# A hybrid attention and convolution backbone on one core: the early output projection one query block sooner with seven row pairs, five convolution chunks on the first token half, and the final norm's weight multiplied ahead of its root

## The chip, the cores and the metric

The kernel runs on one core of a Trainium2 chip. Its engines work side by side, each with a queue of its own: TensorE (PE) for matrix products, VectorE (DVE), ScalarE (ACT) and GpSimd (POOL) for elementwise work, and SyncE (SP), which issues most of the transfers. The metric is the device time of one execution in microseconds; lower is better.

## What is computed

Two layers over 1024 latent tokens of width 1024 with 256 context tokens, cut to what matters here:

```python
# layer 0: windowed attention (|i-j| <= 128) with a sink, gated
h    = rmsnorm(x, g0) * (1 + scale0) + shift0
proj = h @ attn_w_in                      # q, k, v and the gate path z
o    = windowed_attention(rope(q), rope(k), v, k_ctx, v_ctx, sink)
x1   = x + gate0 * ((o * silu(z)) @ attn_w_out)
# layer 1: convolution module, gated
h2   = rmsnorm(x1, g1) * (1 + scale1) + shift1
a, gl, z = split(h2 @ conv_w_in + b, 3)   # three parts of width 2048
u    = depthwise_conv31(a * sigmoid(gl))
u    = silu(layernorm(u))
x2   = x1 + gate1 * ((u * silu(z)) @ conv_w_out)
out  = x2 * rsqrt(mean(x2 * x2) + eps) * final_g
```

Everything is in float32. Each large product is made of three products of float32r parts (high by high, high by low, low by high), so an operand is first split into a high part (a copy on ACT) and a low part (a subtraction on DVE or POOL).

## The kernel before, in words

**The attention.** Sixteen heads with eight query blocks of 128 tokens make 128 steps. In each step PE computes the scores of the next block (`scores`, three times two matmuls), then "fills" with `FILL` = 12 matmuls of other work, then transposes the probabilities of the present block (`transposes`), and after every fourth block multiplies them with the values (`pv`). Between scores and transposes lies the softmax: a masked maximum on DVE (it writes `sc`), the exponential on ACT, a reciprocal on DVE and a multiplication on POOL. The transposed probabilities leave PSUM as `pthi` (ACT) and `ptlo` (DVE). The filling work is taken from a queue, `fillq`: the input projections of later heads, the last of which is the gate path `z` of head 15.

**The early output projection.** The output projection (`proj_attn`) contracts over eight row pairs, a pair being two heads, for four blocks of rows in each of four passes. It needs, for each pair, the weight `wo`, its low part `wol` (made earlier by `low_parts` and kept in DRAM) and the gated head outputs `ozf` read back from DRAM. In head 15 the projection begins early as filling work: at query blocks `EARLY_FROM - 2` and `EARLY_FROM - 1` the loads of the first two pairs are issued, at `EARLY_FROM` their split, and `early_proj` joins the queue, frees the pages of the layer's input and does the first two of the four row blocks for `EARLY_ROWS` pairs, 12 matmuls a pair. The main loop then starts those pairs at the third row block (line 724).

**The way to the convolution.** Behind each pass `evac0` adds the residual and collects sums of squares. When the second half of the tokens (512) is complete, eight closures `turn_in` are put on a list, `later`: each transposes a slice of the normalised rows on PE, and DVE and ACT make `hf`, `h2h` and `h2l` of it, the operands of the next projection.

**The convolution's projection.** `b_mm(i, half)` multiplies chunk `i` (128 output channels) of the weight with one half of the tokens: 24 matmuls of 512 columns. Chunks come in the order gl 0, a 0, gl 1, a 1, gl 2, and so on, with z chunks mixed in from the ninth pair on. Before, chunks 0 to 3 (`2 * EARLY`) run on the first token half, then the same chunks on the second, and from chunk 4 on both halves of a chunk follow each other. While chunks 2 and 3 run on the first half, `b_mm` takes the second half's `turn_in` closures from `later`. A gl chunk goes through a sigmoid into a page that all channel tiles share (`sigp`, one half each for the two token halves); an a chunk is multiplied with it into `ubuf`, where the depthwise convolution reads it (`conv_dve`: 32 products and sums on DVE per channel tile; `conv_pool`: the odd taps, products on ACT, sums on POOL). The layer norm's mean is a matmul of the sum of all channel tiles, `vsum`.

**The final norm.** `evac1` handles one block of 128 rows after the last projection: gate product (DVE, out of PSUM), residual (DVE or POOL), `Square` with its sum on ACT, then, when both column halves are there, `rstd_of`: `ms` (DVE), a square root (ACT) and five small DVE instructions up to `r`. Two DVE instructions multiply each half with `r` and the weight `fg`, and SP stores each half.

**What sets the order.** From line 1064 on only PE keeps the program's order. The order on DVE, ACT, POOL and SP is set when the kernel is built, by a planner that simulates the engines and prefers what stands earlier in the program; the engines then keep to it. Tiles lie in 45 pages of 4 KB a partition, handed out in the order in which they were freed; PSUM has two score tiles, two `psg` banks and two `pso` banks.

Of the kernel before, what the change touches and what calls it, by code (L numbers as in the profile page):

```python
# [11 lines left out]
AF = mybir.ActivationFunctionType  # L12
ALU = mybir.AluOpType
# [20 lines left out]
FILL = 12  # L34
DEFER = 6
EARLY = 2
EARLY_ROWS = 6
EARLY_FROM = 4
KEEP = 8
BYBLOCK = 3  # L40
ZV = (1, 4, 7)
# [52 lines left out]
def backbone_kernel(  # L94
# [8 lines left out]
    V, A, G, PE, SY = (InOrder(tc, e) for e in (nc.vector, nc.scalar, nc.gpsimd, nc.tensor, nc.sync))  # L103
# [29 lines left out]
    def ps_g():  # L133
        return ps.tile([P, 512], F32, tag="g", name=nm("psg"), bufs=2)
# [3 lines left out]
    def ps_og():  # L138
        flip[0] ^= 1
        return ps_o() if flip[0] else ps_g()  # L140
# [4 lines left out]
    def small(shape, dt=F32, name="sm", bufs=2):  # L145
        return cpool.tile(shape, dt, tag=f"{name}", name=nm(name), bufs=bufs)

    def act(out, in_, func, **kw):
        return A.activation(out=out, in_=in_, func=func, **kw)

    def tt(eng, out, a, b, op):
        return eng.tensor_tensor(out=out, in0=a, in1=b, op=op)

    def stt(out, in0, scalar, in1, op0, op1):
        return V.scalar_tensor_tensor(out=out, in0=in0, scalar=scalar, in1=in1, op0=op0, op1=op1)
# [39 lines left out]
    def mm3(o, wh, wl, rh, rl, start, stop):  # L195
        PE.matmul(o, wh, rh, start=start, stop=False)
        PE.matmul(o, wh, rl, start=False, stop=False)
        PE.matmul(o, wl, rh, start=False, stop=stop)
# [293 lines left out]
    for pr in range(NPR):  # L492
        a, b = 2 * pr, 2 * pr + 1
# [143 lines left out]
    def proj_attn():  # L637
# [32 lines left out]
        def ahead(i, nl, ns):  # L670
            while todo["load"] <= min(i + nl, len(seqB) - 1):
                load(todo["load"])
                todo["load"] += 1
            while todo["split"] <= min(i + ns, len(seqB) - 1):
                split(todo["split"])
                todo["split"] += 1

        def block(s, kk, b, acc, w, o):
            for e in range(2):
                lh, ll = (t[:, e, b * P:b * P + P] for t in o)  # L680
                for a, c in ((lh, w[0]), (lh, w[1]), (ll, w[0])):
                    PE.matmul(acc, a, c[:, e], start=kk == 0 and e == 0 and a is lh and c is w[0],
                              stop=kk == NK - 1 and e == 1 and a is ll)
                    yield
# [6 lines left out]
        banks = {4: ps_g(), 5: ps_g()}  # L691
        for i in range(EARLY_ROWS):
            ahead(i, EA, min(1, EARLY_ROWS - 1 - i))
            for b in range(2):
# [7 lines left out]
        for i, (s, kk) in enumerate(seqB):  # L702
# [9 lines left out]
            if i >= len(seqB) - BYBLOCK:  # L712
# [10 lines left out]
                continue  # L723
            for b in range(2 if i < EARLY_ROWS else 0, 4):
                run(block(s, kk, b, acc[b], w, o))
# [192 lines left out]
    def run(gen):  # L918
        for _ in gen:
            pass  # L920
# [12 lines left out]
    def enqueue(key):  # L933
        fillq.append((key, job(key)))
# [148 lines left out]
    for i, (h, qb) in enumerate(steps):  # L1083
        if qb == 0:
            for n in (() if h % 4 == 3 else (h + 1,) if h % 4 or not h else (h, h + 1)):
                enqueue(("z", n))
                if n + 1 < NH:
                    enqueue(("q", n + 1))
        if (h, qb) == (NH - 1, EARLY_FROM - 2):
            run(lows)  # L1090
        if h == NH - 1 and EARLY_FROM - 2 <= qb < EARLY_FROM:
            next(projA)
        if (h, qb) == (NH - 1, EARLY_FROM):
            next(projA)
# [68 lines left out]
    border = []  # L1163
# [35 lines left out]
    def v2(ap):  # L1199
        return ap.rearrange("p (a b) -> p a b", b=256)  # L1200
# [83 lines left out]
    def conv_unit(j, n0, n1, whole=None):  # L1284

        if (j, n0) not in conv:
            st = {"done": False, "us": None, "n0": n0, "n1": whole or n1}
            conv[(j, n0)] = st
            if whole and whole > n1:
                conv[(j, n1)] = st  # L1290
            pq.append(conv_pool(j, n0, whole or n1))
        opened.add((j, n0))
        dq.append(conv_dve(j, n0, n1))
# [13 lines left out]
    def advance(dt):  # L1307
        pump(pq, "p", dt, P_COST)
        pump(dq, "d", dt, D_COST)


    def vh(j, half):
        return vpg[j][:, :, half * 256:half * 256 + 256]
# [46 lines left out]
    late = deque()  # L1360
# [42 lines left out]

    def b_mm(i, half):
        wh, wl = wsB.need(i)
        if i < 2 * EARLY or late:
            o = ps_g()
        else:
            o = ps_og()
        sl = slice(half * 512, half * 512 + 512)  # L1410
        for kt in range(KT):
            mm3(o, wh[:, kt], wl[:, kt], H2h[(half, kt)], H2l[(half, kt)], kt == 0, kt == KT - 1)
            if kt % 2 and later and i >= EARLY:
                later.popleft()()
            if kt == 3:
                advance(2.6)
        kind, j = border[i]
        cur[0] = i
        bias = vt[:, boff[kind] + j:boff[kind] + j + 1]
        if kind == "gl":  # L1420
            with tc.high_priority():
                act(sigt[(j, half)], o, AF.Sigmoid, bias=bias)
        elif kind == "a":
            u = ubuf[j % 4]
            while any(k[0] == j - 4 for k in opened):
                advance(2.6)
            with tc.high_priority():
                stt(u[:, :, 8 + half * 256:264 + half * 256], v2(o), bias, v2(sigt[(j, half)]), ALU.add, ALU.mult)
            if j < EARLY:
                conv_unit(j, *((248, 512) if half else (0, 248)))  # L1430
            elif half:
                conv_unit(j, 0, 512 if j < JSPLIT else 256, 512)
        else:
            zs = zbuf[j % len(zbuf)][:, half]
            with tc.high_priority():
                act(zs, o, AF.Silu, bias=bias)
            if (j, half) in yready:
                tt(V if j % 8 in ZV else G, vh(j, half), vh(j, half), v2(zs), ALU.mult)
            else:
                spilled.add((j, half))  # L1440
                SY.dma_start(out=zsd[j, :, sl], in_=zs)
        late_now()
        if not late:
            advance(2.6)
# [7 lines left out]
    def late_now():  # L1452

        if ("a", NJ - 1) not in border[:cur[0]]:
            return
        late0.append(1)
        if len(late0) == LATE_FROM:
            while dq or pq:
                advance(2.6)
            late.append(1)  # L1460
        if late:
            ln_run(5.2, len(late) in LN_AT)
            late.append(1)
# [4 lines left out]
    def tok_rows(ap, h, b):  # L1468

        n0 = h * 256 + b % 2 * P  # L1470
        return ap.rearrange("(n a) d -> a n d", a=2)[b // 2, n0:n0 + P]
# [29 lines left out]
    def evac1(s, b, acc):  # L1501
        h, m = subs[s]
        ns = slice(m * 512, m * 512 + 512)
        if b % 2 == 0:
            x2[(m, b // 2)] = pg.alloc(F32, [2, 512], "x2")
            x2["xr"] = pg.alloc(F32, [2, 512], "xr")
        if m == 0:
            x2[b] = small([P, 2], name="ssf", bufs=8)
        t, ss, xr = x2[(m, b // 2)][:, b % 2], x2[b], x2["xr"][:, b % 2]
        SY.dma_start(out=xr, in_=tok_rows(x1d, h, b)[:, ns])  # L1510
        tt(V, t, acc, gbc[:, ns], ALU.mult)
        tt(G if b % 2 and s < len(subs) - 1 else V, t, t, xr, ALU.add)
        if b % 2:
            pg.free(x2["xr"])
        junk = hp.alloc(F32, None, "junk")
        act(junk[:, 0:512], t, AF.Square, accum_out=ss[:, m:m + 1])
        hp.free(junk)
        if m == 0:
            return
        tt(V, ss[:, 0:1], ss[:, 0:1], ss[:, 1:2], ALU.add)  # L1520
        r = rstd_of(ss[:, 0:1], D, 1)
        dst = tok_rows(out[0], h, b)
        for m in range(2):
            t = x2[(m, b // 2)]
            os = slice(m * 512, m * 512 + 512)
            stt(t[:, b % 2], t[:, b % 2], r, fg[:, os], ALU.mult, ALU.mult)
            SY.dma_start(out=dst[:, os], in_=t[:, b % 2])
            if b % 2:
                used.append(t)
# [82 lines left out]

    run(projA)
    pg.free(*gbc0)
    for i in range(2 * EARLY):
        b_mm(i, 0)
        wsB.load()
        wsB.split()
        wsB.load()
    for i in range(2 * EARLY):  # L1620
        b_mm(i, 1)
        wsB.done(i)
        wsB.load()
    for i in range(2 * EARLY, len(border)):
        if i == len(border) - 1:
            next(projB)
        wsB.need(i)
        wsB.load()
        wsB.split()
        wsB.load()  # L1630
        b_mm(i, 0)
        if i == len(border) - 1:
            pg.free(*h2pg[0])
            next(projB)
        b_mm(i, 1)
        wsB.done(i)
        if border[i] == ("a", NJ - 1):
            zbuf.append(sigp)
# [3 lines left out]
    fg = pg.alloc(F32, [1024], "fg")  # L1642
# [52 lines left out]
```

## Time and profile before

| | |
|---|---|
| median of 3 runs | 1778.02 us (1777.82 to 1778.15) |
| the profiled execution | 1782.36 us, its span 1780.1 us |
| granted TensorE clock, mean | 0.991 |
| moved by DMA | 242.43 MB, mean 136 GB/s |

The span runs from the first to the last instruction of the profiled execution. All work is recorded under line 88, the helper that issues every instruction, so the profile is read by tile names (`psg`, `h2l_page`, `sc`), engines and time. A row of the timeline has the start, the duration, the engine, the operation, the output and inputs, and in brackets the idle time of the engine before it with what ended it. A matmul's duration overlaps the next one's, so PE's pace is read from start to start. A row of the waits has the total, the number and the longest.

### The profile page before, as it was taken

The numbers are of one execution on the slowest core, as the hardware profiler recorded it, in microseconds if no ns is written. First come the engines' busy times: TensorE is split into PE (matmuls) and PEld (weight loads), VectorE is DVE, ScalarE is ACT, GpSimd is POOL, SyncE is SP. The second block draws the span as 40 slices with busy tenths as digits, with TensorE's granted clock in tenths as the row PEclk, the third lists the DMA queues.
The fourth block names the chain that finished last, engine by engine and source line by source line (L and its number), as shares of the span: only waits on it lengthen the run. The fifth ranks groups of instructions, "written<-read, shape, count | busy, mean of one in ns | idle before, by whom it ended". The sixth has DMA issues, their size and how long they took to land. (4 is left out here: it accounts for less than half of the span.)

```text
span 1780.1 us, 23728 instructions
## 1 busy us (share of the span) xinstructions
PE 1722.9 (97%) x8383; PEld 1419.1 (80%) x8383; DVE 1203.3 (68%) x2165; ACT 885.6 (50%) x1540; POOL 780.4 (44%) x610
## 2 busy tenths in 40 slices
PE   5999999999999999999999999999999999999997
PEld 2788888788887888788888887888888888787886
DVE  6766774667555664666314269999999999866823
ACT  6555543455344453444433445654656565456730
POOL 0244343333423343432100247998988789120300
PEclk8999999999999999999999999999999999999999
DMA  9334443444234443336776733111121212377881
GB/s 311 102 81 139 143 127 93 125 147 145 80 116 131 142 150 93 114 100 206 256 248 241 260 94 102 29 48 36 36 83 36 73 46 71 120 245 237 311 281 48
DMA packets 195322, 242.43 MB, mean 136 GB/s; under 512 B 11798, under 2 KB 126790, under 8 KB 195204
## 3 DMA queue, kind: packets, MB, share of 16 engines
q1 hardware_dynamic: 188516, 230.10, 39.8%
q10 hardware_dynamic: 6688, 10.83, 2.6%
q8 instruction: 66, 1.08, 0.3%
q14 instruction: 52, 0.43, 0.1%
HBM read 188.70 MB, written 41.69 MB: 129 GB/s over the span
## 5 line engine op out<-in xcount | busy, mean ns | idle before, releaser
L88 POOL TENSOR_TENSOR odd_half<-odd_half,prod_half 128x513 f32<-128x513 f32 (+2 forms) x252 | 317.9, 1269 | 20.8 <-ACT prod_half L88 7.3
L88 POOL TENSOR_TENSOR wlo_page<-wraw_page,whi_page 128x1024 fp32r<-128x1024 f32 x71 | 173.8, 2449 | 153.0 <-ACT whi_page L88 115.6
L88 POOL TENSOR_SCALAR p_page<-p_page,sc 128x640 f32<-128x640 f32 (+1 forms) x128 | 104.2, 815 | 307.7 <-DVE sc L88 280.2
L88 PE MATMUL psg<-hh_page,whi_page 128*128 128x512 f32 x600 | 237.6, 396 | 0.0
L88 PE MATMUL psg<-hh_page,wlo_page 128*128 128x512 f32 x600 | 236.3, 394 | 0.0
L88 PE MATMUL psg<-hl_page,whi_page 128*128 128x512 f32 x600 | 236.0, 393 | 0.0
L88 ACT ACTIVATE prod_half<-ubuf,dww 128x513 f32<-128x513 f32 (+2 forms) x252 | 165.0, 674 | 108.6 <-POOL odd_half L88 104.4
L88 PE MATMUL psg<-h2l_page,whi_page 128*128 128x512 f32 x456 | 180.6, 396 | 1.8 <-DVE h2l_page L88 1.8
L88 PE MATMUL psg<-h2h_page,whi_page 128*128 128x512 f32 x456 | 181.5, 398 | 0.0
L88 PE MATMUL psg<-h2h_page,wlo_page 128*128 128x512 f32 x456 | 180.1, 395 | 0.0
L88 DVE SCALAR_TENSOR_TENSOR pss<-ubuf,wsum,pss 128x512 f32<-128x512 f32 (+3 forms) x270 | 172.3, 671 | 0.3
L88 DVE SCALAR_TENSOR_TENSOR pss<-ubuf,dww,pss 128x512 f32<-128x512 f32 (+3 forms) x270 | 172.1, 671 | 0.3
L88 ACT ACTIVATE p_page<-p_page,sc 128x641 f32<-128x641 f32 (+1 forms) x128 | 102.9, 804 | 91.8 <-DVE sc L88 87.3
L88 ACT ACTIVATE pthi<-pss 128x640 fp32r<-128x640 f32 (+1 forms) x144 | 88.7, 616 | 104.7 <-PE pss L88 98.0
L88 DVE TENSOR_TENSOR ptlo<-pss,pthi 128x640 fp32r<-128x640 f32 (+1 forms) x144 | 103.1, 716 | 45.7 <-ACT pthi L88 45.3
L88 PEld LDWEIGHTS psg<-hh_page,wlo_page 128*128 128x128 f32 x600 | 112.8, 188 | 26.2
L88 ACT ACTIVATE whi_page<-wraw_page 128x1024 fp32r<-128x1024 f32 x88 | 92.8, 1054 | 73.9 <-PE psg L88 22.3
L88 PEld LDWEIGHTS psg<-hl_page,whi_page 128*128 128x128 f32 x600 | 112.9, 188 | 20.1
L88 PEld LDWEIGHTS psg<-hh_page,whi_page 128*128 128x128 f32 x600 | 112.8, 188 | 20.0
L88 PE MATMUL pso<-h2l_page,whi_page 128*128 128x512 f32 x312 | 122.9, 394 | 0.0
L88 PE MATMUL pso<-h2h_page,wlo_page 128*128 128x512 f32 x312 | 122.8, 393 | 0.0
L88 PE MATMUL pso<-h2h_page,whi_page 128*128 128x512 f32 x312 | 122.7, 393 | 0.0
(240 smaller groups left out, 4026.8 us busy)
## 6 DMA issues: line engine op xcount, KB each, us to landing
wraw_page<-in_conv_w_in_dram SPq DMA_DIRECT2D x48, 512.0 KB
wraw_page<-in_attn_w_in_dram SPq DMA_DIRECT2D x40, 512.0 KB
wo_page<-in_attn_w_out_dram SPq DMA_DIRECT2D x32, 512.0 KB
wol_page<-wolA SPq DMA_DIRECT2D x32, 512.0 KB
wo_page<-in_conv_w_out_dram SPq DMA_DIRECT2D x32, 512.0 KB
wol_page<-wolC SPq DMA_DIRECT2D x32, 512.0 KB
rope_half<-rope_half ACTq DMA_DIRECT2D x80, 128.0 KB
araw_page<-in_ada_w_dram SPq DMA_DIRECT2D x32, 256.0 KB
```

The lines of the kernel that those rows point to most:

```text
L88: r = f(*a, **k)
```

## The change

```diff
-EARLY_ROWS = 6
-EARLY_FROM = 4
+FIRST = 5
+EARLY_ROWS = 7
+EARLY_FROM = 3
...
     def b_mm(i, half):
         wh, wl = wsB.need(i)
-        if i < 2 * EARLY or late:
+        if i < FIRST or late:
             o = ps_g()
...
         act(junk[:, 0:512], t, AF.Square, accum_out=ss[:, m:m + 1])
         hp.free(junk)
+        tt(V, t, t, fg[:, ns], ALU.mult)
         if m == 0:
             return
...
             os = slice(m * 512, m * 512 + 512)
-            stt(t[:, b % 2], t[:, b % 2], r, fg[:, os], ALU.mult, ALU.mult)
+            if m:
+                V.tensor_scalar(out=t[:, b % 2], in0=t[:, b % 2], scalar1=r, scalar2=None, op0=ALU.mult)
+            else:
+                act(t[:, b % 2], t[:, b % 2], AF.Copy, scale=r)
             SY.dma_start(out=dst[:, os], in_=t[:, b % 2])
...
-    for i in range(2 * EARLY):
+    for i in range(FIRST):
         b_mm(i, 0)
...
-    for i in range(2 * EARLY):
+    for i in range(FIRST):
         b_mm(i, 1)
...
-    for i in range(2 * EARLY, len(border)):
+    for i in range(FIRST, len(border)):
```

It does three things. The early projection enters the filling queue at block 3 of head 15 instead of block 4 (its first loads at blocks 1 and 2, and the flush of remaining low parts at block 1), and does seven row pairs instead of six. Five chunks, not four, run on the first token half before the second half begins. And each half row is multiplied with the final weight right after its squares are summed, so that behind `r` only a scaling by `r` is left: on ACT for the first column half, on DVE for the second.

## The prediction

> **What bounds the kernel now.** I read the page first, then who waited for whom on PE, then the timeline of PE around each long wait, and last the timelines, groups and windows that tell what DVE, ACT and SP do there.
>
> ```profile
> span 1780.1 us, 23728 instructions
> PE 1722.9 (97%) x8383; PEld 1419.1 (80%) x8383; DVE 1203.3 (68%) x2165; ACT 885.6 (50%) x1540; POOL 780.4 (44%) x610
> ...
> DVE  6766774667555664666314269999999999866823
> ```
>
> PE works 97% of the span, so the change can only win where PE stands still or runs slowly: 57 us in all. No matmul is removed. DVE's row matters for a later step: from its 25th slice on it has ten nines, so it is nearly full through the convolution.
>
> ```profile
> PE pss L88 <- DVE sc L88: 5.7, 5, 2.0
> ...
> PE psg L88 <- DVE h2l_page L88: 1.8, 2, 1.4
> ...
> PE pso L88 <- DVE vsum_page L88: 1.0, 1, 1.0
> ...
> PE pso L88 <- DVE r L88: 0.6, 1, 0.6
> ```
>
> The longest single wait inside the attention is 2.0 us, for `sc`. The two waits for `h2l_page` are the second half of the tokens coming late into the convolution's projection. The change aims at these two and at the tail. The last two rows are waits it doesn't touch.
>
> **Early output projection, one block sooner.** First an undisturbed block step of the last head, then the step without filling work.
>
> ```profile
> 838.02 0.71 PE L88 MATMUL pss<-ident,p_page 128*128 128x128 f32 x5
> 838.49 0.42 PE L88 MATMUL pss<-kh_page,qh_page 128*128 128x384 f32 x1
> ...
> 839.45 0.39 PE L88 MATMUL psg<-hh_page,whi_page 128*128 128x512 f32 x1
> ...
> 842.23 0.38 PE L88 MATMUL pss<-ident,p_page 128*128 128x128 f32 x2
> ```
>
> Five transposes take 0.47 us, six score matmuls 0.96, twelve filling matmuls 2.78 (0.232 each): 4.21 a step.
>
> ```profile
> 844.26 0.27 PE L88 MATMUL pss<-kvc_page,ql_page 128*128 128x256 f32 x1
> 846.53 1.30 PE L88 MATMUL pss<-ident,p_page 128*128 128x128 f32 x5 [2.00 <-DVE sc L88]
> 848.31 0.69 PE L88 MATMUL pss<-kh_page,qh_page 128*128 128x384 f32 x1 [0.48 <-DVE ptlo L88]
> ...
> 850.07 0.63 PE L88 MATMUL psg<-woh_page,ozh_page 128*128 128x512 f32 x1
> ...
> 854.23 0.40 PE L88 MATMUL pso<-pthi,kvc_page 128*128 128x512 f32 x1
> ```
>
> The gate path's chunk of head 15 is used up in the step before, and the early projection comes only at query block 4, so at block 3 the transposes stand directly behind the scores. The last score matmul, half as wide as a filling one (0.12 us), leaves PE free at 844.38; the filling work ends at 854.23: 9.85 us for work of 4.21. The loss is 5.6 us, more than the idle 2.48.
>
> ```profile
> 844.00:850.00 6.00, 3.53 (x15) 2.89 (x14) 5.01 (x10) 5.86 (x12) 1.74 (x3) 0.69 1.04 399
> ```
>
> The rest is the clock: the third number from the end, the granted clock, is 0.69 over these six microseconds. The Trainium skill, page "TensorE: Matmul & The Clock Gate", section "What's actually happening", grants half rate only after an idle window of about 3.4 us. By it a pause of 2.0 us would not slow the clock, and closing it would win only the idle time. The trace doesn't agree: two pauses of 2.00 and 0.48 us stand in the stretch with the lowered clock.
>
> With the change twelve matmuls lie between 844.38 and 847.16, past 846.53, when the transposes could start. Nothing is added to PE: the main loop does seven, not six, rows from their third block on, twelve matmuls less. What is late next is the evacuation of the block before:
>
> ```profile
> 847.45 0.80 DVE L88 TENSOR_TENSOR ptlo<-pss,pthi 128x640 fp32r<-128x640 f32 x1
> ...
> 865.27 1.23 DVE L88 TENSOR_TENSOR ozl_page<-ozf_page,ozh_page 128x1024 fp32r<-128x1024 f32 x1 [0.41 <-ACT ozh_page L88]
> ```
>
> `ptlo` is done at 848.25, while the next scores would start at 847.16 + 0.47 = 847.63. I keep 0.6 us for it. So this part wins 5.6 - 0.6 = **5.0 us**. Bounds: 5.6 if DVE's order moves `ptlo` forward; nothing if the new matmuls themselves wait for an operand. For the operands: the seventh pair's low part (`ozl`, the last row) is ready at 866.5 even at the old pace. In the new order steps of 4.21 carry one row pair each, so the seventh starts at 844.4 + 6 x 4.21 = 869.6; the last two steps have no scores (1.9 less, 867.7), and two PV products come on top. So it finds its operands there even unmoved, and the planner is free to move their loads and splits.
>
> ```profile
> L88 SPq DMA_DIRECT2D ozf_page<-ozd x8: 359/374/540, 807.4 to 862.9; - x8
> ...
> 842.28 1.06 ACT L88 ACTIVATE ozh_page<-ozf_page 128x1024 fp32r<-128x1024 f32 x1 [2.80 <-DMA ozf_page<-ozd]
> ```
>
> The first load went out at 807.4, long before the block that issues it in the text, so the moved loads (three transfers a pair on SP, past one block's adaLN loads and the stores of `ozd`) have room. The second row is the danger: ACT waited 2.80 us for a load with the exponential queued behind it, then POOL's normalising and PE's transposes. In full steps a softmax chain has 2.78 + 0.47 + 0.96 + 2.78 = 7.0 us from its scores to its transposes. The chain of block 3 took 846.53 - 839.45 = 7.1 with ACT's 2.80 in it, so one such wait is just covered; a longer one costs a stall as above. The flush of remaining low parts, also moved a block, has nothing left to issue:
>
> ```profile
> L88 SPq DMA_DIRECT2D wolC<-low_page x16: 326/327/432, 449.1 to 778.4; - x16
> ```
>
> **Five chunks on the first half.**
>
> ```profile
> 1074.47 0.40 PE L88 MATMUL psg<-h2h_page,whi_page 128*128 128x512 f32 x1
> 1075.27 0.50 PE L88 MATMUL psg<-h2l_page,whi_page 128*128 128x512 f32 x1 [0.40 <-DVE h2l_page L88]
> ...
> 1077.84 0.50 PE L88 MATMUL psg<-h2l_page,whi_page 128*128 128x512 f32 x1 [1.40 <-DVE h2l_page L88]
> ...
> 1082.05 0.40 PE L88 MATMUL psg<-h2h_page,whi_page 128*128 128x512 f32 x1
> ...
> 1113.46 5.57 PE psg L88 x24
> ```
>
> From 1074.47 to 1082.05 there are 15 matmul places, 3.48 us at 0.232, in 7.58 us: 4.1 us lost, again part of it at half clock. A fifth chunk on the first half (gl of channel tile 2; the last row, from the chain, gives the price of 24 matmuls, 5.57 us) comes before this and is missing later, so PE's sum stays. Then the two waiting matmuls come at 1074.70 + 5.57 = 1080.3 and 1075.4 + 5.57 = 1081.0, behind their data (1075.3 and 1077.8) by 5.0 and 3.1 us. The fifth chunk's weights:
>
> ```profile
> L88 POOL TENSOR_TENSOR wlo_page<-wraw_page,whi_page x6: 2390/2420/2693, 1017.3 to 1044.1; 128x1024 fp32r<-128x1024 f32 x6
> ```
>
> Six chunks were split by 1046.5; the fifth is wanted when the second half starts now, at 1074.47 less 18 places, about 1070. The added sigmoid overwrites a half that the a product has read by then, and the PSUM bank choice only follows. Upper bound 4.1, lower bound 0: PE arrives earlier at the mean of the layer norm, where it already waited 1.0 us for DVE's `vsum`, and DVE is nearly full on the way.
>
> ```profile
> 1078.00:1524.00 446.00, 446.00 (x1921) 362.09 (x1922) 428.18 (x671) 253.28 (x353) 378.57 (x277) 1.00 0.18 55
> ...
> L88 DVE TENSOR_TENSOR wlo_page<-wraw_page,whi_page 128x1024 fp32r<-128x1024 f32 x13 | 21.8, 1675 | 8.6 <-ACT whi_page L88 6.7 <-issue 1.0 <-ACT prod_half L88 0.9
> ...
> L88 DVE SCALAR_TENSOR_TENSOR ubuf<-psg,vt,sig_page 128x512 f32<-128x512 f32 x16 | 12.0, 747 | 5.5 <-PE psg L88 5.5
> ```
>
> DVE has 446 - 428.18 = 17.8 us free, of which 5.5 end with PE and 6.7 with a weight split on ACT, whose queue follows PE too. So DVE can come 4.1 us sooner if PE does. I let 0.5 come back at `vsum`: **3.6 us**.
>
> **The final weight ahead of the root.**
>
> ```profile
> 1770.66 0.69 DVE L88 TENSOR_TENSOR x_page<-x_page,xr_page 128x512 f32<-128x512 f32 x1
> ...
> 1772.22 1.41 DVE L88 SCALAR_TENSOR_TENSOR x_page<-x_page,r,fg_page 128x512 f32<-128x512 f32 x2
> 1773.54 0.15 DVE L88 TENSOR_SCALAR ms<-ssf 128x1 f32<-128x1 f32 x1
> ...
> 1774.79 0.16 DVE L88 TENSOR_TENSOR r<-rr,rq 128x1 f32<-128x1 f32 x1
> ...
> 1776.43 0.33 SPq L88 DMA_DIRECT2D out_dram<-x_page  x1
> ...
> L88 DVE TENSOR_SCALAR xn_page<-x_page,r 128x512 f32<-128x512 f32 x16 | 6.9, 481 | 0.2
> L88 ACT ACTIVATE prod_half<-ubuf,dww 128x513 f32<-128x513 f32 (+2 forms) x252 | 165.0, 674 | 108.6 <-POOL odd_half L88 104.4
> ```
>
> After the last `r` (1774.95) two products in series lead to the last store at 1776.43, 1.48 us on. New: ACT scales one half (0.67 by the last row, plus 0.1 to hand over), DVE the other beside it (0.48); the stores follow at about 0.8 and, one issue of 0.33 later, 1.2. That wins 0.3. Ahead of `r`, `ms` stood 1.32 us behind the former block's two products; now one scaling (0.48) and one new product (0.69, as the first row) stand there, 1.17: 0.2 with rounding up for their overlap. Sum **0.5 us**. Bounds: 1.0 if only the new product stays ahead of `ms`; -0.2 if ACT also runs the former block's copy ahead of the root. Elsewhere 16 products are added on DVE and 8 scalings go to ACT. They hide where DVE and ACT are free (8.5 of 16 and 17.7 of 45 us busy):
>
> ```profile
> 1634.00:1650.00 16.00, 15.44 (x76) 12.61 (x75) 8.54 (x18) 9.89 (x18) 3.21 (x2) 1.00 0.98 351
> 1680.00:1725.00 45.00, 45.00 (x197) 36.74 (x196) 17.70 (x51) 18.40 (x30) 3.51 (x3) 1.00 0.91 314
> ```
>
> Without that cover, four products (2.8 us) would stand before the second half's root, for which PE waits 0.6 already.
>
> **Sum.** 5.0 + 3.6 + 0.5 = 9.1 us. The profiled execution took 1782.36 us (span 1780.1), 4.3 more than the median of the runs, 1778.02; I take the same difference from the median: **1768.9 us**.
>
> **Rivals.** (1) DVE can't follow: all of the 4.1 returns as a wait of some 5 us at `vsum`. For it speak the ten nines, against it the idle time that ends with PE. Gain 5.0 + 0.5: 1772.5. (2) The half clock doesn't come from the pauses and stays where it is: then part one wins 2.48 - 0.6 = 1.9, part two its idle 1.8, less 0.1 at `vsum`, the tail 0.5, together 4.1: 1773.9. This is what the skill's 3.4 us window would make of it; the row of the granted clock speaks against. (3) The early projection doesn't do what it says: the twelve matmuls wait for their split or their bank, and the stall stays. Gain 3.6 + 0.5 = 4.1: 1773.9. Against it stand the early split times. (4) Slower: the splits, a block sooner, put ACT's wait for a load ahead of the exponential in several blocks. Each stall costs 5.6 us with its slow clock; slower by more than 0.2% needs 9.1 + 3.6 = 12.7 us of new loss, so three of them, 16.8: 1785.7. For it speaks the 2.80 us wait; against it, that the loads have no fixed place.
>
> **How the numbers follow.** Chances: my forecast 0.70, rival 1 0.12, rival 2 0.04, rival 3 0.08, rival 4 0.06. The low end takes the bounds together: 5.6 + 4.1 + 1.0, and the wait for `vsum` gone as well (1.0): 11.7, 1766.3. The high end reaches over rivals 1 to 3: 1774.0; rival 4 is left out. About 0.2% (3.6 us, 1774.5) is what a measurement of this kernel can tell from no change. The forecast and rival 1 lie clear of it; rivals 2 and 3, at 4.1, clear it by 0.5 only, so I count 0.04 of the forecast's chance and half of theirs, with some doubt about each, as no change.
>
> **What would show it.** Right: between the scores of blocks 4 and 5 of the last head twelve `psg` matmuls of the early projection at 0.23 us, no granted clock under 1 there; `h2l_page` gone from PE's waits and the fifth chunk before 1075; `vsum` still near 1 us; after the last `r` an ACT and a DVE scaling side by side. Wrong: a new wait of PE for `sc`, `p_page` or `ozl_page` in blocks 1 to 4, or `vsum` at 3 us and more.

## The result, and the profile after

The changed kernel takes 1768.84 us (median, 1766.55 to 1770.29); the kernel before, beside it, 1778.09 us (1777.82 to 1779.23). The ratio is 0.9943 with a 95% interval of 0.9929 to 0.9957. The medians differ by 9.25 us, where 9.1 was forecast; by the ratio it is 10.1 us (7.6 to 12.6). A second timing gave 1768.72 us and a ratio of 0.9942 (0.9930 to 0.9954). The profiled executions differ by more, 1780.1 against 1768.5 us of span, 11.6 us. Of that, 1.0 lies ahead of the first matmul that was moved: the last matmul of the gate path starts at 842.00 us before and at 841.02 after. In the thirteen executions traced for this case, changed or not, it starts anywhere from 838.05 to 842.43. A single pair of executions is therefore read stage by stage, not by its spans.

The page of the changed kernel begins with the span and PE's busy time; from the waits on PE come the three rows behind it (total, count, longest).

```profile
span 1768.5 us, 23741 instructions
PE 1717.3 (97%) x8383; PEld 1415.8 (80%) x8383; DVE 1202.3 (68%) x2173; ACT 890.0 (50%) x1548; POOL 784.0 (44%) x610
```

```profile
PE pss L89 <- DVE sc L89: 3.9, 4, 1.3
...
PE pso L89 <- DVE vsum_page L89: 1.5, 1, 1.5
...
PE pso L89 <- DVE r L89: 0.3, 1, 0.3
```

PE does the same 8383 matmuls in 5.6 us less of busy time, although none was removed: matmuls at the slow clock count as busy, and there are fewer of them. One of the five waits for `sc`, the one of 2.0 us, is gone, and no row names `h2l_page` any more. The wait for `vsum` is 0.5 us longer. (Work is recorded under line 89 now, since one line was added above it.)

Block 3 of the last head, in PE's timeline of the changed kernel (start, duration, operation), and then the busy times and the clock of the window in which the granted clock was 0.69 before:

```profile
843.58 0.28 PE L89 MATMUL pss<-kvc_page,ql_page 128*128 128x256 f32 x1
843.70 0.39 PE L89 MATMUL psg<-woh_page,ozh_page 128*128 128x512 f32 x1
...
846.22 0.39 PE L89 MATMUL psg<-woh_page,ozl_page 128*128 128x512 f32 x1
846.45 0.71 PE L89 MATMUL pss<-ident,p_page 128*128 128x128 f32 x5
846.92 0.42 PE L89 MATMUL pss<-kh_page,qh_page 128*128 128x384 f32 x1
```

```profile
844.00:850.00 6.00, 6.00 (x33) 5.13 (x32) 3.32 (x7) 4.89 (x8) 1.12 (x2) 1.00 1.02 394
```

Between the last score (843.58) and the transposes (846.45) stand twelve matmuls of the early projection at 0.23 us each. Neither the transposes nor the next scores wait, so there is no bracket behind any of these rows, and the clock is 1.00. The DVE timeline says why not even `ptlo` is waited for:

```profile
844.98 0.07 DVE L89 DVE_READ_ACCUMULATOR2_ANT sc<- 128x1 f32 x1
845.31 0.82 DVE L89 TENSOR_TENSOR ptlo<-pss,pthi 128x640 fp32r<-128x640 f32 x1 [0.26 <-ACT pthi L89]
```

`ptlo` ends at 846.13, ahead of the scores at 846.92. In the kernel before, a 1.21 us split of `ozl` stood between `sc` and `ptlo`; with the splits a block earlier, it isn't there. Before:

```profile
846.31 0.07 DVE L88 DVE_READ_ACCUMULATOR2_ANT sc<- 128x1 f32 x1
846.31 1.21 DVE L88 TENSOR_TENSOR ozl_page<-ozf_page,ozh_page 128x1024 fp32r<-128x1024 f32 x1
847.45 0.80 DVE L88 TENSOR_TENSOR ptlo<-pss,pthi 128x640 fp32r<-128x640 f32 x1
```

The end of the changed kernel, in the timeline of DVE, ACT and SP (SP's row is the issue of the last store):

```profile
1760.59 0.49 DVE L89 TENSOR_SCALAR x_page<-x_page,r 128x512 f32<-128x512 f32 x1
...
1760.96 0.71 ACT L89 ACTIVATE x_page<-x_page,r 128x512 f32<-128x512 f32 x1
1761.08 0.69 DVE L89 TENSOR_TENSOR x_page<-x_page,fg_page 128x512 f32<-128x512 f32 x1
...
1761.88 0.15 DVE L89 TENSOR_SCALAR ms<-ssf 128x1 f32<-128x1 f32 x1
...
1763.14 0.16 DVE L89 TENSOR_TENSOR r<-rr,rq 128x1 f32<-128x1 f32 x1
1763.33 0.72 ACT L89 ACTIVATE x_page<-x_page,r 128x512 f32<-128x512 f32 x1 [1.00 <-DVE r L89]
1763.33 0.48 DVE L89 TENSOR_SCALAR x_page<-x_page,r 128x512 f32<-128x512 f32 x1
...
1764.27 0.38 SPq L89 DMA_DIRECT2D out_dram<-x_page  x1
```

The two scalings after the last `r` start at the same moment. From the last `r` to the issue of the last store it was 1.64 us before (1774.79 to 1776.43); now it is 1.13 (1763.14 to 1764.27).

### The profile page after: what moved, and what is told of

Same layout as the page of the kernel before. It is cut to its first block, busy times and chain, and to the rows that moved or that the text cites. A ratio compares the mean times of both kernels' runs of the same rounds, so it can differ in the third digit from the quotient of the medians.

```text
span 1768.5 us, 23741 instructions
## 1 busy us (share of the span) xinstructions
PE 1717.3 (97%) x8383; PEld 1415.8 (80%) x8383; DVE 1202.3 (68%) x2173; ACT 890.0 (50%) x1548; POOL 784.0 (44%) x610
## 4 chain that ended last, share of the span: by engine, by line
PE 82%; DMA 7%; DVE 5%; ACT 2%; issue 1%; POOL 1%; SPq 1%; ACTq 0%; DVEq 0%; POOLq 0%
PE psg L89 42%; PE pss L89 21%; PE pso L89 19%; DMA rope_half<-rope_half 1%; DMA araw_page<-in_ada_w_dram 1%; DMA low_page<-in_conv_w_out_dram 1%; DMA low_page<-in_attn_w_out_dram 1%; DVE low_page L89 1%; DVE ptlo L89 1%; SPq L89 1%; DVE p_page L89 1%; DVE mask_page L89 1%; DVE rope_half L89 1%; ACT lhi_half L89 0%; DMA x_page<-in_x_dram 0%
## 5 line engine op out<-in xcount | busy, mean ns | idle before, releaser
L89 POOL TENSOR_TENSOR odd_half<-odd_half,prod_half 128x513 f32<-128x513 f32 (+2 forms) x252 | 313.9, 1253 | 24.6 <-ACT prod_half L89 11.4
L89 PEld LDWEIGHTS psg<-hh_page,wlo_page 128*128 128x128 f32 x600 | 112.6, 188 | 26.3
```

The source lines that it names most:

```text
L89: r = f(*a, **k)
```

## Where the time went, stage by stage

The same landmarks are taken in the trace of every kernel. A stage is the time between two landmarks; each starts or ends on a PE instruction except the last. "Early" runs from the last gate-path matmul of head 15 to the last matmul of the output projection, "half 1" over the next 64 `h2h_page` matmuls behind the first four chunks (four more chunk halves: 4 x 5.57 = 22.28 where nothing stalls), "convolution" from there to the mean (`vsum`), "tail" from the last matmul to the end of the span.

| kernel (below) | early | half 1 | convolution | tail |
|---|---|---|---|---|
| before | 202.38 | 26.42 | 428.74 | 10.65 |
| after | 196.47 | 22.26 | 428.83 | 10.04 |
| early projection alone | 196.43 | 26.43 | 428.50 | 10.63 |
| five chunks alone | 202.45 | 22.32 | 429.22 | 10.64 |
| final weight alone | 203.76 | 24.87 | 428.74 | 9.77 |
| start at block 3, six pairs | 196.68 | 26.29 | 428.45 | 10.64 |
| seven pairs, start at block 4 | 202.68 | 24.79 | 428.69 | 10.63 |
| twelve useless matmuls | 200.30 | 24.86 | 428.75 | 10.64 |
| five useless matmuls | 200.64 | 26.43 | 428.74 | 10.66 |
| after, once more | 196.44 | 22.27 | 428.83 | 10.05 |
| after, with six chunks | 196.44 | 22.31 | 429.37 | 10.07 |
| after, weight splits on POOL | 196.41 | 22.27 | 427.18 | 9.76 |
| the same, once more | 196.50 | 22.27 | 427.18 | 9.78 |

Each part moves its own stage: early 5.9, half 1 4.15, tail 0.6 in the pair of before and after. The convolution gives 0.1 back in this pair, 0.5 with the chunks alone. Some cells move without being touched. Half 1 takes 26.3 to 26.4 in four of the seven kernels that leave it as it was, and 24.8 to 24.9 in the other three; that is taken up below. The early stage of the final weight alone is 1.4 longer than before: in that execution ACT waited for one more load of `ozf` (1.51 us), so the `ozl` split ahead of `ptlo` came late and PE waited 2.17 us for `ptlo` instead of 0.48. The tail takes 9.76 to 9.78 in three of the six executions with the final weight and 10.04 to 10.07 in the other three.

## The experiments

**The parts one by one.** Early projection alone, in the kernel before:

```
-EARLY_ROWS = 6
-EARLY_FROM = 4
+EARLY_ROWS = 7
+EARLY_FROM = 3
```

> The kernel before with the early output projection alone (seven row pairs, from block 3 on). Theory (the step without filling work cost 5.6 us, idle time and slow clock together, and in the changed kernel the scores behind it no longer wait for ptlo): 5.6 to 5.9 us faster than before, no granted clock under 1 at 842 to 850 us. The prediction's term kept 0.6 us for ptlo: 5.0 faster. Rival (only the idle 2.48 us comes back, the clock slows anyway): 1.9 to 2.5 faster. If the three parts help each other, this one alone gives clearly less than 5.

Measured: 1773.69 us, ratio 0.9969 (0.9956 to 0.9981) to the 1779.2 of before on that chip: 5.5 us less (3.4 to 7.8). The early stage is 5.95 us shorter, with the clock at 1.00 there. The rival's 1.9 to 2.5 lies outside the interval.

Five chunks alone:

```
+FIRST = 5
...
-        if i < 2 * EARLY or late:
+        if i < FIRST or late:
...
-    for i in range(2 * EARLY):
+    for i in range(FIRST):
         b_mm(i, 0)
...
-    for i in range(2 * EARLY):
+    for i in range(FIRST):
         b_mm(i, 1)
...
-    for i in range(2 * EARLY, len(border)):
+    for i in range(FIRST, len(border)):
```

> The kernel before with five chunks on the first token half alone. Theory: the two waits for h2l_page (1.8 us) and the slow clock behind them go, 4.1 us, and 0 to 0.5 comes back at vsum: 3.6 to 4.1 us faster, vsum at 1.0 to 1.5 us. Rival (DVE can't follow): vsum at about 5 us and no gain (0 to 0.5). Rival (the clock doesn't come from the pauses): 1.8 us faster at most.

Measured: 1776.60 us, ratio 0.9980 (0.9971 to 0.9989), by the ratio 3.6 us less (2.0 to 5.2); the medians differ by 2.6. Half 1 takes 4.1 us less, `vsum` is waited for 1.5 us, and the convolution gets 0.5 back. The rival with a wait of 5 us at `vsum` falls. The third, with 1.8 us at most, lies only just outside the interval; the useless matmuls below are needed for it.

Final weight alone:

```
+        tt(V, t, t, fg[:, ns], ALU.mult)
...
-            stt(t[:, b % 2], t[:, b % 2], r, fg[:, os], ALU.mult, ALU.mult)
+            if m:
+                V.tensor_scalar(out=t[:, b % 2], in0=t[:, b % 2], scalar1=r, scalar2=None, op0=ALU.mult)
+            else:
+                act(t[:, b % 2], t[:, b % 2], AF.Copy, scale=r)
```

> The kernel before with the final weight ahead of the root alone. Theory: from the last matmul to the last store 0.5 to 1.1 us less than the 6.9 us of before (the traces of before and after differ by 1.1 there), the rest unchanged: 0.5 to 1.1 faster, at the edge of what the rounds can tell. Rival (the sixteen products on DVE hold up the second half's root and others): the wait for r on PE grows over 0.6 us and the total is 0 to 2 us slower.

Measured: 1778.77 us, ratio 0.9993 (0.9984 to 1.0002): between 2.8 us less and 0.4 more, which the timing alone can't tell from nothing. In the trace the tail is 0.9 us shorter (9.77 against 10.65), and PE has no wait for the second half's `r`, so the rival is not seen here. That wait moves by itself: among the executions with the final weight it is 0.3 us in the changed kernel and 0.9 with six chunks, without it 0.6 before and none with the early projection alone. By the ratios the three parts alone sum to 5.5 + 3.6 + 1.2 = 10.3 us, and together they gave 10.1; by the medians it is 8.5 and 9.25. So nothing shows that the parts help or hinder each other, within intervals of 1.6 us and more to either side.

**Which half of the early projection.** Start at block 3 with six pairs, and seven pairs with the old start:

> The kernel before with the early projection from block 3 on, but still six row pairs. Theory (the gain is the filled step at block 3): the first stall goes, but six pairs of twelve matmuls end one step sooner, so the last step before the main projection has no filling work; the last steps are read from the trace. If that empty step costs as much as the one at block 3, the gain is about 0; if the end of the head has work beside it anyway (no scores, two value products), 3 to 6 us faster.

> The kernel before with seven row pairs, but from block 4 on as before. Theory (the number of rows only moves twelve matmuls from the main loop into the queue): the stall at block 3 stays, and the time is the same as before, within 1 us. Rival (the seventh pair is what wins): 3 us or more faster, with the row of sc in PE's waits unchanged.

Measured: 1773.62 us, ratio 0.9967 (0.9954 to 0.9979), and 1779.19 us, ratio 1.0004 (0.9995 to 1.0013). By the ratios that is 5.9 us less (3.7 to 8.2), and 0.7 more (from 0.9 less to 2.3 more). The earlier start is the whole gain; the seventh pair by itself is nothing, and beside the earlier start it is worth 0.2 us of the stage (196.68 to 196.47). The feared empty step at the other end doesn't show.

**Is it the pause that slows the clock?** Twelve matmuls whose result nobody uses, put where PE stood idle:

```
             scores(*nxt)
+        if (h, qb) == (NH - 1, EARLY_FROM - 1):
+            idle = ps_g()
+            for n in range(12):
+                PE.matmul(idle, qt[h][0][:, 0:P], qt[h][0][:, 0:512], start=n == 0, stop=n == 11)
         if not regroup:
             fill(FILL)
```

> The kernel before with twelve useless matmuls put between the scores and the transposes of block 3 in the last head, where PE stood idle; their result isn't used, nothing is left out and no other work is moved. Theory (the slow clock at 846 us follows from the pauses, so the step loses 5.6 us): the twelve cost 2.78 us of PE and win the 5.6, so 2.2 to 2.8 us faster than before, with no half clock at 846. Rival (the slow clock is there whatever PE does): 2.78 us of work in 2.48 us of idle time, 0.3 to 0.9 us slower than before, and the half clock stays.

Measured: 1778.16 us, ratio 0.9992 (0.9983 to 1.0001), 1.4 us less, between 3.0 less and 0.2 more. The timing alone can't tell that from nothing, though the rival's 0.3 to 0.9 more lies outside the interval. The early stage is 2.1 us shorter in the trace, a little under the 2.2 to 2.8 expected. PE's timeline and the same window as above, for this kernel:

```profile
844.80 2.90 PE L88 MATMUL psg<-qh_page 128*128 128x512 f32 x12
847.53 0.71 PE L88 MATMUL pss<-ident,p_page 128*128 128x128 f32 x5
848.75 0.44 PE L88 MATMUL pss<-kh_page,qh_page 128*128 128x384 f32 x1 [0.51 <-DVE ptlo L88]
```

```profile
844.00:850.00 6.00, 5.49 (x31) 4.68 (x32) 4.92 (x10) 5.77 (x11) 1.75 (x3) 1.00 1.04 402
```

PE does 2.78 us more work here and is done 2.1 us earlier: that can only be if more than the idle 2.48 us was lost before, and the clock, 1.00 instead of 0.69, says what. So the slow clock follows from the pause, not from the place. The 0.51 us for `ptlo` is the wait that the prediction kept 0.6 us for: it does come where the `ozl` split still stands ahead of `ptlo`.

**How long must a pause be?** The records of the clock put every half-clock stretch on a fixed raster: in the kernel before the two behind the start begin at 846.27 and 1078.37, 232.1 us or 68 x 3.413 apart, and last 6.83 and 3.41 us, two steps of it and one. So the busy time of PE (second figure) was read window by window on that raster, with the granted clock third from the end. Before:

```profile
842.85:846.27 3.42, 1.68 (x9) 0.96 (x8) 2.90 (x5) 3.28 (x8) 0.94 (x2) 1.00 1.04 393
846.27:849.68 3.41, 2.68 (x10) 2.30 (x11) 2.42 (x6) 3.41 (x6) 0.80 (x1) 0.50 1.04 401
849.68:853.09 3.41, 3.41 (x11) 2.74 (x10) 2.66 (x5) 2.79 (x5) 1.35 (x2) 0.50 1.05 401
...
1074.96:1078.37 3.41, 1.71 (x5) 0.97 (x6) 3.41 (x9) 2.13 (x4) 3.25 (x4) 1.00 0.28 83
1078.37:1081.78 3.41, 3.41 (x9) 2.65 (x8) 3.41 (x8) 3.41 (x8) 3.18 (x4) 0.50 0.53 154
```

The kernel with the final weight alone, whose half 1 was short:

```profile
1072.19:1075.60 3.41, 3.01 (x14) 2.13 (x12) 3.41 (x5) 2.22 (x6) 3.41 (x2) 1.00 0.91 259
1075.60:1079.01 3.41, 2.00 (x7) 1.19 (x8) 3.41 (x9) 2.39 (x5) 3.17 (x5) 1.00 0.12 32
1079.01:1082.42 3.41, 3.41 (x17) 2.75 (x16) 3.41 (x8) 3.18 (x6) 3.25 (x4) 1.00 0.55 152
```

Both have the same two pauses, 0.40 and 1.40 us. Before, both fall almost wholly into one window (1.70 us idle), and the next window runs at half clock; here an edge of the raster lies between them, 1.41 us is left in the second window, and the clock stays. Over the traces of before, after and the eight experiments above and below that were run up to then, from 70 us on to the tail, every window at full clock with 1.71 us or more of pauses was followed by half clock, and none with 1.55 or less. An experiment was made of it, with five useless matmuls instead of twelve:

> The kernel before with five instead of twelve useless matmuls at block 3 of the last head; their result isn't used, nothing is left out. Theory (in the runs so far a stretch of 3.41 us of PE's clock record is followed by half clock when PE stood still for 1.71 us or more in it, and never when it stood still for 1.55 or less): about 1.3 us of pauses stay (0.85 for sc, 0.48 for ptlo), so no half clock at 846; 1.16 us of added work and 1.3 of pauses in place of 5.6: from the last gate matmul of head 15 to the end of the output projection about 3 us less than before, 0.9 less than with twelve. Rival (any long pause slows the clock): half clock stays, and the stage takes as long as before, within 0.5 us. Rival (only work in the whole gap helps): more than with twelve.

Measured: 1777.47 us, ratio 0.9988 (0.9980 to 0.9997), 2.1 us less (0.5 to 3.6). PE's two pauses and the raster's windows in this kernel:

```profile
843.73 0.74 PE L88 MATMUL pss<-ident,p_page 128*128 128x128 f32 x5 [1.05 <-DVE sc L88]
845.50 0.45 PE L88 MATMUL pss<-kh_page,qh_page 128*128 128x384 f32 x1 [1.04 <-DVE ptlo L88]
```

```profile
841.62:845.03 3.41, 1.79 (x10) 1.07 (x8) 3.41 (x8) 3.04 (x5) 0.94 (x2) 1.00 1.05 406
845.03:848.44 3.41, 2.94 (x15) 2.61 (x16) 2.19 (x4) 3.26 (x5) 0.89 (x2) 1.00 1.03 392
1070.31:1073.72 3.41, 1.78 (x6) 1.01 (x7) 3.41 (x9) 1.96 (x4) 3.17 (x5) 1.00 0.24 72
1073.72:1077.13 3.41, 3.41 (x10) 2.67 (x9) 3.41 (x8) 3.41 (x8) 3.25 (x4) 0.50 0.54 153
```

The sizes came out otherwise than expected: the pauses sum to 2.09 us, not 1.3, and the stage won 1.7 us, not 3, and no more than with twelve. But the clock stayed at 1.00, since the edge of a window at 845.03 divides the two pauses into 1.62 and 0.47. The same run has, at 1070.31, a window with 1.63 us of pauses that is followed by half clock. So the border lies at about 1.6 us, near half of a window; the ends of matmuls are modelled, so it can't be read to a hundredth. The rival by which any long pause slows the clock falls, here by the place of that edge: 2.09 us in one window would lie above the border.

**Is the fifth chunk only the cover for `h2l_page`?** Six instead of five, in the changed kernel:

> The changed kernel with six instead of five chunks on the first token half. Theory (the fifth chunk won only the two waits for h2l_page and their slow clock, which are gone): no difference to the changed kernel, within 1 us, so again 8.5 to 9.5 us faster than before. Rival (more work ahead of the second half helps by itself, by way of DVE's or POOL's lead): another 1 us or more. A loss of 1 us or more would say that the sixth chunk's weights or pages come late.

Measured: 1770.53 us, ratio 0.9951 (0.9938 to 0.9963), 8.7 us less than before (6.6 to 11.0). Half 1 takes 22.31 us against 22.26, and the convolution 0.5 more. With the wait gone there is nothing more to win.

**What stands before `vsum`.** In the changed kernel, DVE's timeline ahead of PE's 1.5 us:

```profile
1509.14 1.23 DVE L89 TENSOR_TENSOR wlo_page<-wraw_page,whi_page 128x1024 fp32r<-128x1024 f32 x1 [1.77 <-ACT whi_page L89]
...
1513.59 0.69 DVE L89 TENSOR_TENSOR vsum_page<-vsum_page,v_page 128x512 f32<-128x512 f32 x1
```

DVE stands 1.77 us before a weight split, for ACT's half of it, with the last sums for `vsum` queued behind. The split was given to POOL, which has no work there:

```
-    wsB = WStream(hp=True, lo_eng=lambda i: V if i % 3 == 0 and i > 3 else G, ...
+    wsB = WStream(hp=True, lo_eng=lambda i: V if i % 3 == 0 and 3 < i < 42 else G, ...
```

> The changed kernel with the low parts of the weight chunks 42 and 45 made on POOL instead of DVE. Theory (PE's 1.5 us at vsum come from DVE standing 1.8 us before such a split, for ACT's high part, with the sums for vsum queued behind it): the wait for vsum falls under 0.5 us, and the kernel is 1.0 to 1.5 us faster than the changed one. Rival (vsum is bound by DVE's and POOL's convolution work itself): the wait stays over 1 us and the time is the same; if POOL is late with its own sums, slower.

> The changed kernel once more, beside the next one on the same chip: 8.5 to 9.5 us faster than before, with the wait for vsum at 1.5 us.

> The changed kernel with the low parts of chunks 42 and 45 on POOL, beside the changed kernel on the same chip. Theory (the wait for vsum is gone and nothing new stands in its place): 1.0 to 1.7 us faster than the changed kernel, 10 to 11 faster than before. Rival (the 1.65 us that its trace gains up to vsum come back behind it): no difference to the changed kernel, within 0.5 us.

Measured: 1766.72 us, ratio 0.9931 (0.9917 to 0.9944); and on one chip the changed kernel 1768.72 us, 0.9942 (0.9930 to 0.9954), this one 1767.23 us, 0.9938 (0.9924 to 0.9952). In both executions PE's wait for `vsum` is gone, and from the 601st `h2h_page` matmul to `vsum` it is 263.64 us against 265.29 in both of the changed kernel, 1.65 less. The timing doesn't settle it. On the one chip the medians differ by 1.5 us in the expected direction, but the two ratios by 0.0004 alone, 0.7 us, and their intervals overlap. (The changed kernel itself came out 10.3 us under before there by its ratio, 8.2 to 12.5, a little past the 8.5 to 9.5 expected.) So the cause of the wait is shown, and the faster kernel is likely, not shown.

## Why the prediction was right, point by point

**The stall of block 3: right, and a little more.** Forecast 5.0 us; the stage gave 5.9, and the timing of this part alone 5.5 (3.4 to 7.8). That the loss is idle time plus slow clock, the point on which the term hung, is shown by the useless matmuls: with work in the gap the granted clock goes from 0.69 to 1.00. The 0.6 us kept for `ptlo` is the part that failed. The prediction took DVE's order as it was and named the upper bound of 5.6 for the case that the order moves `ptlo` forward; that is what happened, because the split of `ozl` that stood ahead of it moved too. PE's timelines also show what the 5.9 is made of. From the last gate-path matmul to the last value product of the head PE takes 31.21 us instead of 33.84, with the twelve filling matmuls (2.78) more in it. So about 5.4 come from the stall itself: 5.6, less 0.23 for a new wait for `mask_page`. The rest comes behind it: from there to the end of the projection stand 744 matmuls instead of 756, and they take 165.26 us instead of 168.53. That is 3.27 less, where twelve at 0.223 are 2.68; the others run 0.6 us quicker in all, 0.222 us each instead of 0.223. Why is open.

**Five chunks: the right size, from two values.** Forecast 3.6, as 4.1 less 0.5 at `vsum`; the timing gave 3.6 (2.0 to 5.2). The 4.1 is what the one execution before showed. Seven executions with the waits in place took about 26.4 four times and about 24.8 three times, so the part is worth 4.1 or 2.5 us, by where the raster of the clock falls on the two pauses. The forecast read a price off one throw of that, and the throw was the dearer one; that the size came out right is in part luck. What came back was 0.1 to 0.5 us of the convolution stage, and the wait for `vsum` went from 1.0 to 1.5 us, where the forecast's sign was "still near 1 us".

**The final weight: the step ahead of `r` was mis-sized.** Forecast 0.5: 0.3 behind the last `r`, 0.2 ahead. Behind it came 0.51 (1.64 to 1.13). Ahead of it, from the last residual sum to the last `r`, it was 4.13 us before (1770.66 to 1774.79) and is 3.53 now (1759.61 to 1763.14): 0.6. The prediction let the former block's scaling stand ahead of `ms`; the timeline shows it at 1760.59, beside `Square` on ACT, so only the product of 0.69 stands there, the case of the upper bound of 1.0. Of these 1.1 us 0.6 reached the end of the span: between the issue of the last store and the end of the span lie 4.22 us now, 3.72 before. Both last stores are issued 0.42 us apart instead of 0.66. That can't be all of it: in all six executions with the final weight they are 0.42 to 0.43 apart, and the rest behind them is 3.94 to 3.96 us in three and 4.22 to 4.26 in three, against 3.71 to 3.73 in the seven without. The cause stays open.

**The rivals.** DVE could follow (the wait for `vsum` is 1.5, not 5 us). The early matmuls had their operands: PE shows no wait between 838 and 877 us in the changed kernel's head 15 other than 0.2 for `mask_page`. ACT's waits for the loads of `ozf` were there, 10.9 us in four of them with 4.8 the longest against 8.6 in three before, but none reached PE as a stall. The second rival, by which pauses of 2.0 us leave the clock alone, falls with the useless matmuls. It took up the Trainium skill, page "TensorE: Matmul & The Clock Gate", section "What's actually happening", with its idle window of about 3.4 us. The same section of the Trainium skill says that this window runs freely; the raster of 3.413 us agrees. What fell is only the reading that PE must stand still for all of it: a window with half of it idle, 1.7 us, was enough in the kernel before.

**The sum.** 9.1 was forecast, 9.25 measured in the medians and 10.1 by the ratio (7.6 to 12.6). By the stages and the ratios the terms were 0 to 0.9 too low each; by the medians the chunks alone gave 2.6, 1.0 less than forecast. All of that is well inside the intervals. One sentence of the prediction was too narrow: the 57 us in which the change could win are the time in which PE stands still, while matmuls at the slow clock count as busy, and part of the gain came out of them.

## What to carry to other kernels

A short pause of PE has two prices: its own length, and half a window of slow clock (1.7 us of work lost in 3.4) if enough pauses fall into one window. Its own length is more than the wait row says: where the clock stayed at 1.00, the two pauses of 1.8 us for `h2l_page` cost about 2.5 us. Part of that is that the row begins at the end of a matmul's record, 0.40 us behind its start, where the next could start after 0.23. So price a stall by matmul places lost, not by the wait row, and look at more than one execution, as the second price depends on where the window falls. When filling work is moved earlier, follow everything that moves with it on the other engines: here DVE's split left the place ahead of `ptlo` and removed the wait that was expected next.

## What the runs showed of the hardware

In these traces the granted clock changes only on a raster of 3.413 us. It doesn't move within an execution, and from one execution to another it lies differently against the start of the span. About 1.6 us of pauses in a window, in one piece or several, made the next one half speed: over all thirteen traces, from 70 us to the last matmul, thirteen full-speed windows with 1.62 us or more were followed by half clock, one with 1.62 was not, and none with 1.55 or less was. Five of the traces have such a slow window where nothing was changed, four near 737 us (behind 1.77 to 1.92 us of pauses) and one at 352 (behind 2.04). A slow window with pauses was followed by another (2.68 us busy of 3.41 at 846.27, half clock again); one with 0.15 us of pauses, or none, was followed by full speed. One window doesn't fit: in the changed kernel 57.8 to 61.2 us had only 0.86 us of pauses and was followed by half clock. It also held eight matmuls of 2 columns; whether these count as little work was not tried.

Beside POOL's weight split at 1510.37 (2.40 us), DVE's last sum for `vsum` took longer in the kernel with the split moved, 1.80 us in both of its executions:

```profile
1511.51 1.80 DVE L89 TENSOR_TENSOR vsum_page<-vsum_page,v_page 128x512 f32<-128x512 f32 x1
```

Without POOL beside it the same instruction takes 0.69 us. The wait for `vsum` went all the same: DVE's queue lost the 1.77 us in which it stood still and the split of 1.23 us, more than the 1.1 us added here.
